# A higher rank for mLSTM work in the emission order of a hybrid decoder step

## The chip, the cores and the metric

The kernel runs on one core of a Trainium2 chip. The metric is the device time of one execution in microseconds, from the program's first to its last instruction with what the launch adds around it. "Before" was run three times; one more execution was recorded by the profiler.

## The reference

One layer of an autoregressive decoder is computed for a prompt of 512 positions and for 8 samples of one position each, 520 rows in all, with shared weights:

```
z = rmsnorm(h) @ w_in                      # 1024 -> 8456 columns
o_a = dilated sliding-window attention(z)  # 12 heads; samples read cached keys and values
o_b = mlstm(conv(z)) * sigmoid(z_o)        # 4 heads of 256; samples carry a state C of 256 x 256
h += (sig(g_a) * (o_a @ w_proj_a) + sig(g_b) * (o_b @ w_proj_b)) @ w_out
h += (silu(x @ w_gate) * (x @ w_up)) @ w_down        # x = rmsnorm(h)
h += sigmoid(rmsnorm(h) @ w_ple_gate) * (p @ w_ple_proj)
y = rmsnorm(h)
```

Outputs are y, the new key and value caches, the convolution rows, and the mLSTM state (C, n, m) of prompt and samples. For one sample and head the new state is C' = x·C + k (w v)ᵀ, and the numerator of its output is C'ᵀ q. The output o_b of a head needs the prompt half (512 columns) and the sample half (8 columns).

## The kernel before, in words

All 520 rows stand on the free axis, split in two halves of 260 columns, and features stand on the partitions. Each weight tile of 128 x 128 is split into a rounded part and a remainder (`whi` by ACT or DVE, `wlo` by DVE), and each activation likewise, so that one product is three matmuls. The weights of the projections stream through in a fixed order of chunks (`order`): the columns of `w_in` (attention of the first head pair, mLSTM head 0, attention of the second pair, heads 1 to 3, output gates, then the gate columns g), then `w_proj_a` and `w_proj_b`, `w_out`, and the feed-forward part. `w_proj_b` and most of the feed-forward part use a seven-product block scheme (`wino`), whose right sides are sums of halves of two activation tiles. The tiles that hold them are called `piece`; for `w_proj_b` the four mLSTM heads give them, one after the other (`mk_ob`), and the first block product walks through all four heads.

Everything beside the dense products is written as Python generators. Each yields a condition (`on(engine, tiles, rooms)`: the engine's queue reaches not more than LIM past TensorE's, the tiles are ready, buffers of the named tags are free), by a clock that the kernel keeps while it emits instructions. This clock has costs of its own: a transfer, for one, is taken to land 2.0 us after its turn on the queue. `Procs.run()` is called several times in each chunk of the dense work. In such a turn it goes through the list of evacuations (`evs`) and then through the list `live`, each from its front, and lets each generator go on as long as its condition holds. Weight splits (`feed`) come before it in the turn. So the place in the list decides who takes a free place on an engine; the engines' own queues then run in the order of emission.

The list `live` in the kernel before, from the front: first norm, attention chain of the prompt (`attn_prompt(0)`, then `(1)`; its eight units each are spawned while it runs and go to the end of the list), the mLSTM prompt chain (`mlstm_prompt(0)` to `(3)`), the sample attention (`samples`), the samples' loads (`loads`, head by head; head 0 first, heads 1 to 3 after the sample attention has issued its last value loads, flag `vs`), `sample_rows`, `mlstm_sample`, then `mk_oa` and `mk_ob` (spawned before the dense work starts), and behind them whatever is spawned later: attention units, the two step generators of each head (`steps(0)` for even samples, `steps(1)` for odd ones), `sample_sums`, and the stores of results.

For one mLSTM head the sample half goes so: `sample_rows` writes q and k of the 8 samples to DRAM (`mdr`). `sample_loads` loads q and k of a pair of samples back, spread over the partitions, into one buffer of P1 and one of P2 (`qb`, `kb`; each tag has 2 buffers), and for each sample the state `ct` into one of the 5 buffers of S. A step scales `ct` (ACT or DVE), adds k·v (`ct<-kb,vw,ct`, DVE, twice), multiplies by q and sums (`junk<-ct,qb` into `numv`, DVE, twice), and stores `ct`. When both samples of a pair are done their P1 and P2 buffers come free for the next pair but one. After 8 samples `sample_sums` and `sample_out` multiply the head's tanh gates `th` by `numv`. The prompt half ends with the product `th<-th,hm`. With both, `mk_ob` scales `th` and makes the head's pieces; for head 3 it needs all 5 buffers of S.

P1 and P2 serve attention too: each unit keeps its scores `P` there. Later the gate columns g of two of every four rounds go to P1 and P2, and their evacuation waits until the loads of head 3 have all been issued:

```
if tag in ("P1", "P2"):
    yield lambda: ("loads", 3) in flag
```

All operations are recorded by one helper, so every row of the profile has line 225; rows are told apart by tiles.

Of the kernel before, what the change touches and what calls it, by code (L numbers as in the profile page):

```python
# [229 lines left out]
def _body(nc, a, const, sb, psp, drp):  # L230
# [10 lines left out]
    def tl(tag, name, shape=None, dt=F32):  # L241
        w = WIDTH.get(tag, 520)
        if tag in used:
            used[tag] += 1
        return ck.new(sb.tile(list(shape or (128, w)), dt, name=name, tag=tag, bufs=NB[tag]), tag, NB[tag])
# [8 lines left out]
    def bank(shape=(128, 512)):  # L254
        used["b1"] += 1
        return ck.new(psp.tile(list(shape), F32, name="b1", tag="b1", bufs=4), "b1", 4)
# [7 lines left out]
    def free(n, tag):  # L264
        used[tag] -= n
# [5 lines left out]
    def on(engs, *tiles, lim=None, **rooms):  # L271

        engs = engs.split()

        def ok():
            for tag, n in rooms.items():
                if tag in used and used[tag] + n > NB[tag]:
                    return False
            now = ck.t["pe"]
            for tag, n in rooms.items():  # L280
                i = ck.count.get(tag, 0)
                if any(ck.idle(tag, i + j, NB[tag]) > now + P["SLACK"] for j in range(n)):
                    return False
            if engs[0] == "pe":
                t = now
            else:
                t = min(ck.t[e] for e in engs)
                if t > now + (P["LIM"] if lim is None else lim):
                    return False
                t = max(t, now) + 0.1  # L290
            return all(ck.ready(x) <= t for x in tiles)
        return ok

    class Cycle:
        def __init__(self, tags):
            self.tags, self.i = tags, 0

        def next(self, n):
            return [self.tags[(self.i + k) % len(self.tags)] for k in range(n)]
# [4 lines left out]

    class Procs:
        def __init__(self):
            self.evs, self.live = [], []

        def spawn(self, gen, first=False):
            (self.evs if first else self.live).append([None, gen])  # L310

        def run(self):
            for q in (self.evs, self.live):
                for p in list(q):
                    while p[0] is None or p[0]():
                        try:
                            p[0] = next(p[1])
                        except StopIteration:
                            q.remove(p)
                            break  # L320

    pr = Procs()
# [24 lines left out]
    def pick(names, op, out, ins):  # L347
        def end(n):
            aps = [out] + ins
            s, cost = ck.start(n, [out], ins), ck.cost(n, op, out, aps, ())  # L350
            if ck.shares(n, op, aps):
                s, _ = ck.port(s, cost)
            return s + cost + (P["BIAS"] if n == "dve" else 0.0)
        return min(names, key=end)
# [3 lines left out]
    def copy(dst, src, names=("act", "dve")):  # L358
        n = pick(names, "tensor_copy", dst, [src])
        if n == "act":  # L360
            S_.copy(dst, src)
        else:
            ENG[n].tensor_copy(dst, src)
# [5 lines left out]
    def stt(dst, x, sc, y, op0, op1):  # L369
        V.scalar_tensor_tensor(dst, x, sc, y, op0=op0, op1=op1)  # L370
# [956 lines left out]
    def sample_rows(h):  # L1327

        yield lambda: all(("k", h, dt) in ml for dt in range(2)) and "rows" in flag
        yield on("pe", qkm, b1=1, S=1)  # L1330
        bk = bank((8, 2, 2, 128))
        rows = tl("S", "mrows", (8, 2, 256))
        for w in range(2):
            for dt in range(2):
                PE.transpose(bk[:, w, dt], qkm[:, h, w, dt], ident)
        yield on("act dve", bk)
        copy(rows.rearrange("b w d -> b (w d)"), bk.rearrange("b w t d -> b (w t d)"))
        free(1, "b1")
        yield on("sp", rows)
        dr = drp.tile([8, 2, 256], F32, name="mdr", tag="mdr", bufs=2)  # L1340
        SP.dma_start(dr.rearrange("b w d -> b (w d)"), rows.rearrange("b w d -> b (w d)"))
        free(1, "S")
        mdr[h] = dr
# [18 lines left out]
    def mlstm_sample(h):  # L1362
        yield lambda: (h, 0) in cts and all(("v", h, vt) in ml for vt in range(2))
        yield on("dve", vm, s24b)
        vw = sb.tile([128, 2, 8], F32, name="vw", tag="vw", bufs=2)
        V.tensor_tensor(vw, vm[:, h], s24b[:, h, 8:16].unsqueeze(1).to_broadcast([128, 2, 8]), op=ALU.mult)
        numv = sb.tile([128, 2, 8], F32, name="numv", tag="numv", bufs=2)
        left = [8]

        def steps(b0):  # L1370
            for b in range(b0, 8, 2):
                yield lambda: (h, b) in cts
                cur = cts.pop((h, b))
                qb, kb = qks[h, b - b % 2]
                yield on("act dve", cur, s24b)
                if pick(("act", "dve"), "tensor_scalar", cur, [cur]) == "act":
                    S_.activation(cur, cur, AF.Copy, scale=s24b[:, h, b:b + 1])
                else:
                    V.tensor_scalar(cur, cur, s24b[:, h, b:b + 1], None, op0=ALU.mult)
                for vt in range(2):  # L1380
                    yield on("dve", cur, kb, vw)
                    stt(cur[:, vt], kb[:, b % 2], vw[:, vt, b:b + 1], cur[:, vt], ALU.mult, ALU.add)
                for vt in range(2):
                    yield on("dve", cur, qb)
                    V.tensor_tensor_reduce(junk, cur[:, vt], qb[:, b % 2], 1.0, 0.0, ALU.mult, ALU.add,
                                           numv[:, vt, b:b + 1])
                left[0] -= 1
                done[b] = True
                if b ^ 1 in done:
                    free(1, "P1")  # L1390
                    free(1, "P2")
                store(a["C_s"][h, b], cur, lambda: free(1, "S"))

        done = {}
        for b0 in range(2):
            pr.spawn(steps(b0))
        yield lambda: left[0] == 0
        pr.spawn(sample_sums(h, numv))

    def sample_sums(h, numv):  # L1400

        nn = nout[:, h, :, 1:9]
        w_i = s24b[:, h, 8:16].unsqueeze(1).to_broadcast([128, 2, 8])
        w_x = s24b[:, h, 0:8].unsqueeze(1).to_broadcast([128, 2, 8])
        nt = small(32, "nt").rearrange("p (t c) -> p t c", t=2)
        tv = nt[:, :, 0:8]
        V.tensor_tensor(tv, qkm[:, h, 1], w_i, op=ALU.mult)
        V.tensor_tensor(nn, nst[:, h], w_x, op=ALU.mult)
        V.tensor_tensor(nn, nn, tv, op=ALU.add)
        V.tensor_tensor(tv, nn, qkm[:, h, 0], op=ALU.mult)  # L1410
        V.tensor_tensor(nt[:, :, 8:16], numv, numv, op=ALU.mult)
        yield on("pe", nt, b1=1)
        bk = bank((128, 16))
        for t in range(2):
            PE.matmul(bk, ones, nt[:, t], start=t == 0, stop=t == 1)

        dn = sb.tile([128, 16], F32, name="dns", tag="dns", bufs=2)
        yield on("act", bk)
        S_.activation(dn[:, 0:8], bk[:, 0:8], AF.Abs)
        V.tensor_copy(dn[:, 8:16], bk[:, 8:16])  # L1420
        free(1, "b1")
        yield on("dve", dn)
        V.tensor_tensor(dn[:, 0:8], dn[:, 0:8], s24b[:, h, 16:24], op=ALU.max)
        ml["ns", h] = True
        yield lambda: ("og", h, 0) in ml and ("og", h, 1) in ml
        yield from sample_out(h, numv, dn)
# [163 lines left out]
    def chain(*gens):  # L1590
        for g in gens:
            yield from g
# [113 lines left out]
    def loads():  # L1706
        for c in "0a123":
            if c == "a":
                yield lambda: "vs" in flag
            else:  # L1710
                yield from sample_loads(int(c))
# [4 lines left out]
    for c in "apm":  # L1716
        if c == "a":
            pr.spawn(chain(attn_prompt(0), attn_prompt(1)))
        elif c == "p":
            pr.spawn(chain(*[mlstm_prompt(h) for h in range(4)]))  # L1720
        else:
            pr.spawn(samples())
            pr.spawn(loads())
            pr.spawn(chain(*[sample_rows(h) for h in range(4)]))
            pr.spawn(chain(*[mlstm_sample(h) for h in range(4)]))

    oa = []

# [393 lines left out]
    for h in range(2):  # L2122
        pr.spawn(last_norm(h))
    dense_to(len(order))
    while pr.evs or pr.live:
        stall()
    while copies:
        cache_copy()
# [141 lines left out]
```

## Time and profile before

| | |
|---|---|
| three runs | 1102.45, 1105.98, 1107.39 us; median 1105.98 |
| the profiled execution | 1104.25 us, span 1102.5 us from first to last instruction |
| TensorE busy | 1050.2 us |
| DVE busy | 859.1 us |
| ACT busy | 522.8 us |
| mean granted clock of TensorE | 0.979 of full speed |

Times in the rows are microseconds from the span's start. PE is TensorE's matmul, PEld its weight load, DVE VectorE, ACT ScalarE, SPq the queue on which SyncE issues transfers. A row of a timeline has start, length, engine, line, operation, out<-in with shapes, and the count of merged instructions; in brackets stands the engine's idle time just before and what ended it. The granted clock is 1.00 at 2.4 GHz and 0.50 at 1.2 GHz.

### The profile page before, as it was taken

To read this page: it belongs to the slowest core of one execution; us is meant where nothing else is said; L and a number is where in the kernel's file an instruction comes from. 1 tells how busy PE (TensorE), PEld (TensorE's weight loads), DVE (VectorE), ACT (ScalarE), POOL (GpSimd) and SP (SyncE) were. 2 spreads that over 40 slices of the span, in tenths; PEclk is the share of its full clock that TensorE was granted. 3 is DMA by queue.
4 is the path that set the end of the run, shared out by engine and by line. 5 is a ranking of instruction groups with operands and counts; after the bars stand their busy time and mean duration, and the time that the engine had idled before them with its cause. 6 is when DMAs were issued, how large, how long until landed. Compare 5 with 4: busy or idle time off the path is not lost.

```text
span 1102.5 us, 21771 instructions
## 1 busy us (share of the span) xinstructions
PE 1050.2 (95%) x8404; PEld 1026.4 (93%) x8404; DVE 859.1 (78%) x1768; ACT 522.8 (47%) x968; POOL 35.8 (3%) x126
## 2 busy tenths in 40 slices
PE   7999999999998999997999999989999999999995
PEld 6999899999998989996999999989999999999995
DVE  7994559877778599876466868999888888866775
ACT  6445444664454487754343335435344434433553
POOL 0010010001001011000000000000000000000000
PEclk9999999999997999998999999999999999999998
DMA  6365157747846986876566833322323332333321
GB/s 229 118 201 174 58 193 244 269 150 227 269 138 218 309 268 197 268 213 227 197 210 233 283 103 96 121 84 92 103 83 108 111 101 83 110 94 97 120 83 59
DMA packets 90904, 180.21 MB, mean 163 GB/s; under 512 B 11604, under 2 KB 37252, under 8 KB 89392
## 3 DMA queue, kind: packets, MB, share of 16 engines
q1 hardware_dynamic: 90800, 178.82, 50.5%
q8 instruction: 66, 1.08, 0.4%
q14 instruction: 38, 0.31, 0.1%
HBM read 163.65 MB, written 59.13 MB: 202 GB/s over the span
## 4 chain that ended last, share of the span: by engine, by line
PE 67%; DVE 15%; DMA 8%; ACT 5%; issue 3%; SPq 1%; POOL 0%; DVEq 0%; ACTq 0%
PE pp L225 42%; PE b L225 25%; DVE wlo L225 3%; DMA raw<-in_w_in 3%; DVE yc L225 2%; ACT whi L225 2%; DMA out_C_s<-ct 1%; DMA ct<-in_sC 1%; DMA qb<-mdr 1%; DVE ct L225 1%; SPq L225 1%; DVE junk L225 1%; DVE piece L225 1%; DVE sw L225 1%; DVE h L225 1%
## 5 line engine op out<-in xcount | busy, mean ns | idle before, releaser
L225 DVE TENSOR_TENSOR wlo<-raw,whi 128x512 fp32r<-128x512 f32 (+3 forms) x358 | 236.6, 664 | 148.1 <-ACT whi L225 134.5
L225 ACT CAST whi<-raw 128x512 fp32r<-128x512 f32 (+3 forms) x340 | 203.1, 601 | 290.8 <-PE pp L225 155.3
L225 PE MATMUL b<-piece,whi 128*128 128x260 f32 x1232 | 229.3, 287 | 10.0 <-ACT piece L225 6.0
L225 PE MATMUL pp<-xnh,whi 128*128 128x260 f32 x1008 | 209.4, 289 | 0.8 <-ACT th L225 0.8
L225 PE MATMUL pp<-xnh,wlo 128*128 128x260 f32 x1008 | 208.4, 288 | 0.0
L225 PEld LDWEIGHTS b<-piece,whi 128*128 128x128 f32 x1232 | 194.5, 193 | 12.1 <-ACT piece L225 6.7
L225 PE MATMUL pp<-xnl,whi 128*128 128x260 f32 x1008 | 204.8, 285 | 0.8 <-DVE xnl L225 0.7
L225 PE MATMUL b<-piece,wlo 128*128 128x260 f32 x616 | 176.7, 287 | 0.1
L225 PEld LDWEIGHTS pp<-xnh,whi 128*128 128x128 f32 x1008 | 157.4, 191 | 2.2 <-ACT th L225 1.0
L225 PEld LDWEIGHTS pp<-xnl,whi 128*128 128x128 f32 x1008 | 157.9, 191 | 1.2 <-DVE xnl L225 1.2
L225 PEld LDWEIGHTS pp<-xnh,wlo 128*128 128x128 f32 x1008 | 157.4, 191 | 1.1
L225 PEld LDWEIGHTS b<-piece,wlo 128*128 128x128 f32 x616 | 118.6, 193 | 0.6 <-DVE wlo L225 0.6
L225 PE MATMUL pp<-hpl,whi 128*128 128x260 f32 x352 | 70.8, 282 | 0.0
L225 PE MATMUL pp<-hph,whi 128*128 128x260 f32 x352 | 70.8, 282 | 0.0
L225 PE MATMUL pp<-hph,wlo 128*128 128x260 f32 x352 | 70.7, 282 | 0.0
L225 PEld LDWEIGHTS pp<-hpl,whi 128*128 128x128 f32 x352 | 54.2, 188 | 0.0
L225 PEld LDWEIGHTS pp<-hph,wlo 128*128 128x128 f32 x352 | 54.2, 188 | 0.0
L225 PEld LDWEIGHTS pp<-hph,whi 128*128 128x128 f32 x352 | 54.2, 188 | 0.0
L225 ACT CAST whi<-ws 128x512 fp32r<-128x512 f32 x29 | 17.9, 621 | 57.1 <-PE b L225 48.5
L225 DVE TENSOR_TENSOR uv<-uv,b 128x260 f32<-128x260 f32 (+1 forms) x88 | 42.7, 485 | 0.0
L225 DVE SCALAR_TENSOR_TENSOR yc<-zc,par,yc 128x552 f32<-128x552 f32 x48 | 37.8, 788 | 5.0 <-ACT yc L225 4.5
L225 PE MATMUL pp<-mix,whi 128*128 128x260 f32 x256 | 41.1, 282 | 0.0
(383 smaller groups left out, 1875.3 us busy)
## 6 DMA issues: line engine op xcount, KB each, us to landing
raw<-in_w_in SPq DMA_DIRECT2D x132, 256.0 KB, 3.5
out_kvout<-in_cache SPq DMA_DIRECT2D x64, 512.0 KB, 4.6
raw<-in_w_gate SPq DMA_DIRECT2D x44, 256.0 KB, 3.6
raw<-in_w_up SPq DMA_DIRECT2D x44, 256.0 KB, 4.4
ct<-in_sC SPq DMA_DIRECT2D x32, 256.0 KB, 6.6
out_C_s<-ct SPq DMA_DIRECT2D x32, 256.0 KB, 4.4
raw<-in_w_down SPq DMA_DIRECT2D x32, 256.0 KB, 2.6
out_kvout<-in_cache SPq DMA_DIRECT2D x16, 510.0 KB, 4.9
```

The source lines that it names most:

```text
L225: fn(*args, **kw)
```

## The change

The scheduler gets a third list, `urgent`, between the evacuations and `live`. The prompt chain, the samples' loads, rows and per-head chain, the step generators and the samples' sums are spawned into it. The sample attention, the attention chain and its units, `mk_oa`, `mk_ob` and the stores stay in `live`. Within `urgent` the order is: prompt chain, loads, rows, per-head chain, then steps and sums as they are spawned.

```diff
     class Procs:
         def __init__(self):
-            self.evs, self.live = [], []
-
-        def spawn(self, gen, first=False):
-            (self.evs if first else self.live).append([None, gen])
+            self.evs, self.urgent, self.live = [], [], []
+
+        def spawn(self, gen, first=False, urgent=False):
+            (self.evs if first else self.urgent if urgent else self.live).append([None, gen])
 
         def run(self):
-            for q in (self.evs, self.live):
+            for q in (self.evs, self.urgent, self.live):
...
         for b0 in range(2):
-            pr.spawn(steps(b0))
+            pr.spawn(steps(b0), urgent=True)
         yield lambda: left[0] == 0
-        pr.spawn(sample_sums(h, numv))
+        pr.spawn(sample_sums(h, numv), urgent=True)
...
         elif c == "p":
-            pr.spawn(chain(*[mlstm_prompt(h) for h in range(4)]))
+            pr.spawn(chain(*[mlstm_prompt(h) for h in range(4)]), urgent=True)
         else:
             pr.spawn(samples())
-            pr.spawn(loads())
-            pr.spawn(chain(*[sample_rows(h) for h in range(4)]))
-            pr.spawn(chain(*[mlstm_sample(h) for h in range(4)]))
+            pr.spawn(loads(), urgent=True)
+            pr.spawn(chain(*[sample_rows(h) for h in range(4)]), urgent=True)
+            pr.spawn(chain(*[mlstm_sample(h) for h in range(4)]), urgent=True)
...
-    while pr.evs or pr.live:
+    while pr.evs or pr.urgent or pr.live:
         stall()
```

## Rows read from the trace of the kernel before

**Rows 1.** The page, part 1: busy time, share of the span, instructions.

```profile
PE 1050.2 (95%) x8404; PEld 1026.4 (93%) x8404; DVE 859.1 (78%) x1768; ACT 522.8 (47%) x968; POOL 35.8 (3%) x126
```

**Rows 2.** Busy time by stretch: length, engines (instructions), granted clock, DMA share, GB/s.

```profile
440.00:450.00 10.00, 10.00 (x78) 9.74 (x77) 7.15 (x18) 6.11 (x12) 0.00 (x0) 1.00 1.00 346
...
490.00:497.50 7.50, 7.50 (x65) 7.50 (x64) 1.85 (x3) 1.49 (x3) 0.00 (x0) 1.00 0.77 210
...
514.00:526.10 12.10, 9.18 (x39) 7.86 (x40) 9.13 (x17) 4.69 (x9) 0.00 (x0) 0.58 0.26 87
...
497.50:530.50 33.00, 24.94 (x164) 22.79 (x163) 20.86 (x55) 14.24 (x26) 0.00 (x0) 0.84 0.54 185
530.50:556.50 26.00, 26.00 (x219) 26.00 (x218) 12.62 (x21) 10.32 (x18) 0.00 (x0) 1.00 0.77 272
```

**Rows 3.** Waits from 497 to 531 us: total, times, longest.

```profile
PE b L225 <- ACT piece L225: 4.7, 2, 2.8
...
PE pp L225 <- ACT th L225: 2.6, 3, 1.0
```

**Rows 4.** Timeline of PE: first product on pieces, and the last that waited.

```profile
510.28 0.40 PE L225 MATMUL b<-piece,whi 128*128 128x260 f32 x2
...
522.90 0.59 PE L225 MATMUL b<-piece,whi 128*128 128x260 f32 x1 [0.15 <-DVE piece L225]
```

**Rows 5.** Timeline of SP's queue: second and last pair of head 3.

```profile
451.62 0.38 SPq L225 DMA_DIRECT2D qb<-mdr  x1
...
491.45 1.45 SPq L225 DMA_DIRECT2D qb<-mdr  x1
```

**Rows 6.** Timeline of DVE: steps of heads 2 and 3, and their gate products.

```profile
415.86 0.36 DVE L225 CUSTOM_DVE_ANT_0 junk<-ct,qb 128x256 bf16<-128x256 f32 x1
...
432.57 0.42 DVE L225 CUSTOM_DVE_ANT_0 junk<-ct,qb 128x256 bf16<-128x256 f32 x1
...
465.37 1.67 DVE L225 SCALAR_TENSOR_TENSOR ct<-kb,vw,ct 128x256 f32<-128x256 f32 x4
...
483.79 0.42 DVE L225 CUSTOM_DVE_ANT_0 junk<-ct,qb 128x256 bf16<-128x256 f32 x1
...
484.13 0.68 DVE L225 SCALAR_TENSOR_TENSOR th<-th,hm 128x512 f32<-128x512 f32 x1
...
507.18 0.42 DVE L225 CUSTOM_DVE_ANT_0 junk<-ct,qb 128x256 bf16<-128x256 f32 x1
...
512.41 0.24 DVE L225 SCALAR_TENSOR_TENSOR th<-th,numv 128x8 f32<-128x8 f32 x2
```

**Rows 7.** Tile ct: duration ns min/median/max, first and last start.

```profile
L225 DVE SCALAR_TENSOR_TENSOR ct<-kb,vw,ct x64: 384/479/491, 167.7 to 504.4; 128x256 f32<-128x256 f32 x64
L225 DVE CUSTOM_DVE_ANT_0 junk<-ct,qb x64: 360/422/428, 169.7 to 507.2; 128x256 bf16<-128x256 f32 x64
...
L225 ACT ACTIVATE ct<-ct,s24b x31: 705/722/730, 163.9 to 501.4; 128x512 f32<-128x512 f32 x31
...
DMA to landing us min/median/max: 2.1/6.0/7.2
```

**Rows 8.** Tile piece alone, by stretch: length, PE, PEld, DVE, ACT.

```profile
460.00:470.00 10.00, 0.00 (x0) 0.00 (x0) 3.57 (x7) 0.93 (x2) 1.00 0.56 183
470.00:480.00 10.00, 0.00 (x0) 0.00 (x0) 2.56 (x5) 0.62 (x1) 1.00 0.73 220
```

**Rows 9.** Tiles P and qb: attention's scores, the sample attention's key products.

```profile
L225 DVE CUSTOM_DVE_ANT_0 P<-b,cstA x32: 284/418/425, 92.5 to 244.0; 128x256 f32<-128x256 f32 x28, 128x128 f32<-128x128 f32 x4
...
L225 DVE TENSOR_TENSOR kvb<-kvb,qb x12: 679/684/693, 244.5 to 301.1; 128x512 f32<-128x512 f32 x12
```

**Rows 10.** Timeline of ACT: waits for transfers at the head of its queue.

```profile
364.10 1.40 ACT L225 ACTIVATE ct<-ct,s24b 128x512 f32<-128x512 f32 x2 [2.85 <-DMA out_C_s<-ct]
...
448.42 0.62 ACT L225 CAST whi<-raw 128x512 fp32r<-128x512 f32 x1 [3.21 <-DMA raw<-in_w_in]
```

**Rows 11.** Busy time by stretch, as rows 2: the costliest stall before 400 us.

```profile
345.00:355.00 10.00, 6.87 (x37) 6.35 (x37) 9.37 (x23) 4.77 (x9) 0.41 (x1) 0.67 0.30 108
```

## The prediction

> **What bounds the kernel now.** I read the page's busy times first: TensorE (PE) is recorded busy for 95% of the span [rows 1], so a gain can come only from the few stretches in which it stands or runs slowly. The busy times by stretch find the one that this change can reach. Between 497.5 and 530.5 us TensorE gets through 164 matmuls in 33.0 us; in the 26.0 us behind it, with the same kind of work (gate columns, two short products, seven block products), 219 [rows 2]. That is 26.0 / 219 = 0.1187 us each, and 164 × 0.1187 = 19.5 us: the stretch loses 33.0 − 19.5 = **13.5 us**. Part of it is standing still: three waits of 2.6 us together for ACT's `th` and two of 4.7 us for ACT's `piece` [rows 3]. The rest is mainly clock: behind the long wait, from 514 to 526.1 us, the granted clock is 0.58 on average, mostly its lower level of 1.2 GHz, and 39 matmuls take 12.1 us [rows 2].
>
> The timelines then tell who is late. TensorE reaches the first product on `piece` at 510.28 us and gets the last piece that it lacks at 522.90 [rows 4]. The pieces are those of the fourth mLSTM head, and they wait for its sample half: the last sample's `junk` (the numerator) is made at 507.18, the tanh gates are multiplied by it at 512.41 [rows 6], then scaling and splitting take to 522.90. Before it stands a load: the last pair of samples is issued on the SP queue at 491.45, where the second pair went at 451.62 [rows 5]. That issue needs a buffer of P1 and one of P2, which come free when both samples of an earlier pair are done. The second pair's update (`ct<-kb,vw,ct` x4) ran at 465.37, but its last `junk`, a 0.42 us instruction that needs nothing more, ran at 483.79 [rows 6]: 17 us in which the step was passed over. The three `th` waits are of the same origin: tanh gates that go to P1 and P2 may not be evacuated before the loads of head 3 are all issued.
>
> **The change part by part.** No instruction is added or removed; only the order of emission can differ.
>
> *Prompt chain, sample rows, loads.* In the list of before they stand behind the first norm, the attention chain and (all but the prompt chain) the sample attention, but ahead of the attention units, which are spawned later and go to the list's end. What they are lifted over is seldom alive beside them: attention's `P` is written from 92.5 to 244.0 and the sample attention's key products run from 244.5 to 301.1 [rows 9], while the chain of waits of interest begins after 430. Cost taken: 0 us, with a reason for no large sign: where nobody else has a condition that holds, rank decides nothing. The SP issues of the loads pass only the sample attention's, which end before head 1's loads start by the code's own condition (`vs`).
>
> *Steps.* They stood at the list's end, behind `mk_oa` and `mk_ob`, which are spawned at the start and come alive when the last head's projections are done. Now they go ahead of both. A step is one scaling (0.72 us on ACT), two updates (0.48 us) and two `junk` (0.42 us) with two 0.08 us read-outs: 2 × 0.48 + 2 × 0.42 + 0.16 = 2.0 us of DVE [rows 7]. What they pass between 460 and 480 us is pieces of heads 1 and 2, 3.57 + 2.56 = 6.1 us of DVE [rows 8], besides their sums `ta` and `tb`. These pieces are not wanted before 507; moved back, they are hidden by DVE's idle time from 490 to 497.5, where it is busy 1.85 of 7.5 us [rows 2]. Without that cover they would stall TensorE by up to their 6.1 us, which I keep as a bound.
>
> *What the last pair gains.* From its issue to TensorE's release it is 522.90 − 491.45 = 31.4 us. TensorE without the three `th` waits would want the pieces at 510.28 − 2.6 = 507.7, so the issue must come by 476.3 for the whole stall to go. If the steps win only the time of the pieces that they pass, the issue moves to 491.45 − 6.1 = 485.4, and the release to 516.8: the low bound. If the second pair's `junk` follow its updates as soon as DVE has a place, they end near 469 instead of 484.2, the issue comes near 470, and the release near 501.4: the stall is gone. I take the second, since at 465 to 484 the steps' only rivals above them besides the pieces are the prompt chain's own end and the weight splits, and both go on anyway.
>
> *What is late next.* The prompt half of head 3: its last gate product stands at 484.13 (0.68 us long) [rows 6]. From there scaling and pieces, which took 522.90 − 512.41 = 10.5 us in the sample's case, end at 495.3, still 12 us ahead of 507.7. So TensorE itself is next.
>
> *Loads that come earlier.* A pair is four transfers of 256 KB, pulled forward into a stretch where the DMA engines are already full: share 1.00 from 440 to 450 [rows 2]. There ACT waited 3.21 us for a weight tile at 448.42 [rows 10], and TensorE was busy 10.00 of 10 us all the same [rows 2]. Cost taken 0; upper bound one stall as from 345 to 355 us, where 37 matmuls were done in 10 us instead of 10 / 0.1187 = 84: 47 × 0.1187 = 5.6 us, lower clock included [rows 11].
>
> Sum: −13.5 us, plus 1.5 us that I leave for the new hand-overs (half of the 3 us by which the waits for ACT there could come back), = **−12 us**.
>
> **A rule weighed.** Rows 1 name TensorE as the busiest engine by far. The Trainium skill, Perfetto Trace Analysis, section Identifying the Most-Contended Engine, says to improve the engine of highest occupancy first; by it a new order of DVE and ACT work would leave 1104 us. The same page's section Optimization Strategy asks for the gaps of the regime in question and for what blocks there, and by it the stall is fair game; the rows of the stretch agree with the second.
>
> **The rivals.**
> *Half of it: the top ranks hold the steps.* Evacuations, weight splits and the prompt chain stay ahead. For it: between 415.86 and 432.57 two neighbouring `junk` lie 16.7 us apart [rows 6], before any piece is written. Against it: that was the convolutions' time, and their evacuations end around 430. Then only the 6.1 us of the low bound are won: 1104.25 − 6.1, about 1098 us.
>
> *Nothing.* The last pair stays behind the same weight loads on the SP queue, or another late thing (the pieces of heads 0 to 2, now behind the steps) takes the stall's place in full. Against it, the 12 us of room above. Time 1104 to 1106 us.
>
> *Slower: waits at the head of the queues.* The emission's clock reckons that a transfer lands 2.0 us after its time on the queue; `ct` landed after 6.0 us (median) and up to 7.2 [rows 7]. A step of the last rank was put in its queue late, when the data was there; one of a higher rank is put in at once and stands there, with weight splits behind it. At 364.10 such a scaling held ACT for 2.85 us, put down to the store that its buffer waited for [rows 10]. The place is 440 to 480 us, four pairs, and a stall of TensorE costs 5.6 us [rows 11]. From 12 / 5.6 = 2.1 stalls on the gain is eaten; with all four, 22.4 − 12 = +10, 1115 us. Against it: steps of heads 1 and 2 ran without a competitor from the list and so were put in at once too, and ACT's waits there delayed TensorE little. The Trainium skill (Perfetto Trace Analysis, Tensor Engine Instruction) calls ACT and DVE strict FIFOs, which this mechanism needs; ACT's wait at 448.42 agrees.
>
> **How the numbers follow.** The profiled execution took 1104.25 us (span 1102.5); 1104.25 − 12 = 1092.3. The median of the three runs is 1.7 us higher, which gives 1094.0; I say 1093. Chances: whole stall gone 0.60 (1088 to 1097), half 0.16 (about 1098), nothing 0.13 (1104 to 1106), slower 0.11 (1107 to 1115). The range 1087 to 1107 leaves out only most of the last case and the best ends of the first. About 0.5%, 5.5 us, is what a measurement can tell. Below 1100.5 lie the first case and most of the second: faster 0.70; what is left of the second and the third: same 0.19; slower 0.11.
>
> **What would show it.** Right: stretches up to 430 us nearly as before; the last `qb<-mdr` issued before 476 instead of 491; the last gate product with `numv` before 495; the first product on pieces near 508 with no wait over 1 us behind it and no lower clock up to 530; everything later shifted by some 12 us. Half: that issue near 485, and a wait for `piece` of 5 to 9 us. Slower: waits of ACT or DVE for `ct` of 2 us and more between 440 and 480, with a lower clock there. I should be wrong if the order changes before 300 us, where I found nobody to be passed, or if a weight tile comes too late for TensorE in the fuller DMA stretch.

## The result, and the profile after

| | before | after |
|---|---|---|
| median of 4 runs | 1105.58 us (1102.45 to 1107.39) | 1088.82 us (1087.17 to 1090.90) |
| profiled execution | 1104.25 us, span 1102.5 | 1088.87 us, span 1087.1 |
| mean granted clock | 0.979 | 0.991 |

The ratio is 0.9855, 95% interval 0.9834 to 0.9877: faster by 1.45%, 16 us of 1105.58. The same changed kernel in a second job gave 1094.12 us against 1107.55, ratio 0.9882 (0.984 to 0.9925), and three parts measured beside it are read against that.

First the page of after, busy time by engine, to be held against [rows 1].

```profile
PE 1039.2 (96%) x8404; PEld 1016.2 (93%) x8404; DVE 859.3 (79%) x1772; ACT 520.2 (48%) x964; POOL 37.0 (3%) x126
```

The 8404 matmuls are the same, and their recorded busy time has fallen by 1050.2 − 1039.2 = 11.0 us. So most of the 15.4 us by which the span is shorter had been counted as work of TensorE. That fits the lower clock, of which there is less: a mean of 0.979 over 1102.5 us stands for 46 us at 1.2 GHz, 0.991 over 1087.1 us for 20.

The same stretches as [rows 2, 11] show where.

```profile
345.00:355.00 10.00, 4.59 (x21) 4.32 (x22) 9.77 (x29) 4.10 (x7) 0.41 (x1) 0.56 0.28 93
...
440.00:450.00 10.00, 10.00 (x79) 9.74 (x80) 8.33 (x30) 7.06 (x12) 0.00 (x0) 1.00 1.02 331
...
490.00:497.50 7.50, 7.50 (x65) 7.50 (x64) 6.33 (x14) 6.47 (x12) 0.00 (x0) 1.00 0.66 198
...
497.50:530.50 33.00, 33.00 (x277) 33.00 (x277) 20.75 (x36) 12.29 (x22) 0.00 (x0) 1.00 0.62 214
...
530.50:556.50 26.00, 26.00 (x220) 26.00 (x218) 17.65 (x31) 9.61 (x19) 0.00 (x0) 1.00 0.69 233
...
514.00:526.10 12.10, 12.10 (x103) 12.10 (x103) 9.22 (x16) 4.14 (x7) 0.00 (x0) 1.00 0.71 240
```

The stretch from 497.5 to 530.5 holds 277 matmuls where it held 164, at a clock of 1.00, as dense as the one behind it (33.0 / 277 = 0.119 us each; 26.0 / 220 = 0.118). From 514 to 526.1 it is 103 in place of 39. DVE's idle time from 490 to 497.5 is mostly used up: it is busy 6.33 us of 7.5 where it was 1.85. The stretch from 345 to 355 is still bad, with 21 matmuls at a clock of 0.56 where there were 37 at 0.67.

Then the sample half of head 3: the timeline of SP's queue, second and last pair [rows 5], and of DVE [rows 6].

```profile
441.35 0.57 SPq L225 DMA_DIRECT2D qb<-mdr  x1
...
461.43 0.58 SPq L225 DMA_DIRECT2D qb<-mdr  x1
```

```profile
454.96 1.66 DVE L225 SCALAR_TENSOR_TENSOR ct<-kb,vw,ct 128x256 f32<-128x256 f32 x4
...
457.62 0.41 DVE L225 CUSTOM_DVE_ANT_0 junk<-ct,qb 128x256 bf16<-128x256 f32 x1
...
459.42 0.43 DVE L225 CUSTOM_DVE_ANT_0 junk<-ct,qb 128x256 bf16<-128x256 f32 x1
...
473.74 1.66 DVE L225 SCALAR_TENSOR_TENSOR ct<-kb,vw,ct 128x256 f32<-128x256 f32 x4
...
478.07 0.36 DVE L225 CUSTOM_DVE_ANT_0 junk<-ct,qb 128x256 bf16<-128x256 f32 x1
...
487.89 0.68 DVE L225 SCALAR_TENSOR_TENSOR th<-th,hm 128x512 f32<-128x512 f32 x1
...
488.93 0.24 DVE L225 SCALAR_TENSOR_TENSOR th<-th,numv 128x8 f32<-128x8 f32 x2
```

The second pair's `junk` now stand right behind their updates (454.96, then 457.62 to 459.42), and the last pair is issued 2 us later, at 461.43 instead of 491.45. Its updates run at 473.74, its last `junk` at 478.07, and the gates of head 3 are multiplied by `numv` at 488.93 instead of 512.41, 1 us behind the last product of the prompt half (487.89). TensorE's timeline, first product with `oah` and first with `piece`:

```profile
502.84 0.40 PE L225 MATMUL pp<-oah,whi 128*128 128x260 f32 x2
...
505.71 0.40 PE L225 MATMUL b<-piece,whi 128*128 128x260 f32 x2
```

TensorE waits for nothing at all from 497 to 531 us, where [rows 3, 4] had waits for `th` and `piece`. The chain of work that ended last (start, length, link) agrees. Its longest link outside TensorE behind 460 us is a state on its way in; short links on ACT and DVE follow, the last of them at 479.55, and from there to the block products TensorE stands in the chain alone.

```profile
462.57 7.37 DMA ct<-in_sC
...
479.55 0.18 DVE nt L225
...
480.39 25.48 PE pp L225 x212
505.88 10.05 PE b L225 x84
```

Three milestones divide the difference of the spans. Up to the first product with `oah` it is 502.8 − 505.7 = −2.9 us; from there to the first product with `mix`, behind all block products of `w_proj_b`, 603.4 − 502.8 = 100.6 against 618.9 − 505.7 = 113.2, that is −12.6; from there to the end 483.7 against 483.6.

### The profile page after: what moved, and what is told of

Its sections match the earlier page's. It is cut to its first block, busy times and chain, and to the rows that moved or that the text cites. A ratio compares the mean times of both kernels' runs of the same rounds, so it can differ in the third digit from the quotient of the medians.

```text
span 1087.1 us, 21770 instructions
## 1 busy us (share of the span) xinstructions
PE 1039.2 (96%) x8404; PEld 1016.2 (93%) x8404; DVE 859.3 (79%) x1772; ACT 520.2 (48%) x964; POOL 37.0 (3%) x126
## 4 chain that ended last, share of the span: by engine, by line
PE 69%; DVE 16%; DMA 7%; ACT 4%; issue 3%; SPq 1%; POOL 0%; DVEq 0%; ACTq 0%
PE pp L225 45%; PE b L225 24%; DVE wlo L225 3%; DMA ct<-in_sC 2%; DVE yc L225 2%; DVE ct L225 1%; ACT whi L225 1%; DMA raw<-in_w_in 1%; DMA out_C_s<-ct 1%; SPq L225 1%; DVE junk L225 1%; DMA kvb<-in_cache 1%; DMA out_kvout<-in_cache 1%; DVE sw L225 1%; DVE Wf L225 1%
## 5 line engine op out<-in xcount | busy, mean ns | idle before, releaser
L225 PE MATMUL b<-piece,whi 128*128 128x260 f32 x1232 | 224.5, 284 | 4.6 <-DVE piece L225 1.5
L225 PEld LDWEIGHTS b<-piece,whi 128*128 128x128 f32 x1232 | 190.9, 189 | 5.4 <-issue 2.0
## 6 DMA issues: line engine op xcount, KB each, us to landing
out_kvout<-in_cache SPq DMA_DIRECT2D x64, 512.0 KB, 5.1
```

The lines of the kernel that those rows point to most:

```text
L225: fn(*args, **kw)
```

## The experiments

Each run also shows one profiled execution. For all of them the same two numbers are taken from its timelines: the *lead*, from the issue of the last `qb<-mdr` to the first product with `piece`, and the *stretch*, from that product to the first with `mix`.

| kernel | ratio to before, 95% interval | issue | first `piece` product | lead | stretch |
|---|---|---|---|---|---|
| before | 1 | 491.45 | 510.3 | 18.8 | 108.6 |
| hold_late | 0.9978 [0.9949, 1.0007] | 492.85 | 513.5 | 20.7 | 103.8 |
| ob_urgent | 0.9920 [0.9902, 0.9938] | 484.98 | 506.4 | 21.4 | 105.1 |
| no_steps | 0.9978 [0.9948, 1.0008] | 484.74 | 506.3 | 21.6 | 105.8 |
| hold_3 | 0.9867 [0.9823, 0.9910] | 479.95 | 506.4 | 26.4 | 98.5 |
| hold_mid | 0.9873 [0.9834, 0.9911] | 484.40 | 514.4 | 30.0 | 99.4 |
| chain_first | 0.9909 [0.9884, 0.9934] | 469.11 | 505.8 | 36.7 | 100.1 |
| ob_last | 0.9912 [0.9880, 0.9943] | 478.04 | 519.7 | 41.7 | 99.0 |
| rows_live | 0.9865 [0.9831, 0.9899] | 465.52 | 508.9 | 43.4 | 97.5 |
| after_again | 0.9882 [0.9840, 0.9925] | 465.16 | 509.2 | 44.0 | 98.5 |
| after | 0.9855 [0.9834, 0.9877] | 461.43 | 505.7 | 44.3 | 97.7 |
| prompt_steps | 0.9898 [0.9856, 0.9941] | 462.01 | 509.8 | 47.8 | 97.6 |
| steps_first | 0.9927 [0.9899, 0.9955] | 468.69 | 516.7 | 48.0 | 98.6 |
| prompt_live | 1.0017 [0.9998, 1.0036] | 462.94 | 516.1 | 53.2 | 106.2 |

**Are the steps the cause?** In no_steps they stay in `live`, and all else is promoted.

```diff
-            pr.spawn(steps(b0), urgent=True)
+            pr.spawn(steps(b0))
```

> Changed kernel, but the two step generators of each head stay at the end of the live list (behind mk_oa and mk_ob); prompt chain, loads, rows, per-head chain and sums stay promoted. Theory (the gain is the steps' place ahead of the pieces of heads 0 to 2): the stall before the first block products returns, the last qb<-mdr is issued near 490 us again, waits for ACT piece of 4 us and more with a lower clock behind them, total 1100 to 1105 us. Rival A (the gain comes from the other promotions, or from stores being seen in the same turn): the stall stays away, 1087 to 1091 us. Rival B (any reshuffle of the order moves the stall by chance): anywhere between, with the last issue at a place that has nothing to do with the pieces.

Measured: 1104.22 us (1097.14 to 1109.06), nearly all of the gain gone. The profiled execution is the fastest of the ten; in it the last pair goes out at 484.74 and not near 490 as expected, and the waits for pieces sum to 3.4 us and not to 4 and more. SP's and TensorE's timelines show the last pair and two of these waits.

```profile
484.74 0.42 SPq L225 DMA_DIRECT2D qb<-mdr  x1
...
509.05 0.39 PE L225 MATMUL b<-piece,whi 128*128 128x260 f32 x1 [1.42 <-DVE piece L225]
...
512.40 0.59 PE L225 MATMUL b<-piece,whi 128*128 128x260 f32 x1 [0.87 <-DVE piece L225]
```

**Is it the place relative to the pieces?** In ob_last nothing is promoted, but `mk_oa` and `mk_ob` go to a list of their own behind `live`; in ob_urgent all is promoted as in the change, and these two also, ahead of the steps.

```diff
# ob_last, against before
-            for q in (self.evs, self.live):
+            for q in (self.evs, self.live, self.late):
...
-    pr.spawn(mk_oa())
-    pr.spawn(mk_ob())
+    pr.spawn(mk_oa(), late=True)
+    pr.spawn(mk_ob(), late=True)
# ob_urgent, against after
-    pr.spawn(mk_oa())
-    pr.spawn(mk_ob())
+    pr.spawn(mk_oa(), urgent=True)
+    pr.spawn(mk_ob(), urgent=True)
```

> Kernel before with one thing else: mk_oa and mk_ob go to a third list behind live, so that the steps pass them although nothing is promoted. Theory: this alone gives the gain, 1088 to 1093 us, last qb<-mdr near 462 to 470 us, no wait for piece over 1 us before 570 us; the order up to 430 us is that of before. Rival A (other promotions): 1102 to 1106 us. Rival B (chance): between.

> Changed kernel with mk_oa and mk_ob promoted too; being spawned before the steps they stand ahead of them again, while everything else is as in the changed kernel. Theory: the steps are passed over between 460 and 484 us as before, the last qb<-mdr comes after 480 us, total 1098 to 1104 us. Rival A: 1087 to 1091 us.

Measured: 1096.89 us (1094.14 to 1107.77) and 1098.07 us (1096.38 to 1099.07), against 1106.25. To move two generators back wins 9 us without any promotion, of the 16 and 13 that the changed kernel won in its two jobs, and its stretch is as short as that of after. It was expected at 1088 to 1093 us with the issue at 462 to 470. Its profiled execution is the slowest of the ten and has head 3's write of q and k (`mdr<-mrows`) at 442.65 instead of 427.04; counted from that write the issue comes after 35.4 us, as in after (34.4) and not as in before (58.8). Where the rest of the gain stays is open. To move the two up in the changed kernel brings the issue back to 484.98 and the stretch to 105.1.

**Is it the date of the last pair?** hold_late, hold_3 and hold_mid keep the order of the changed kernel and hold only the last pair's loads until the loads of weights have come to a given chunk.

```diff
                 yield on("sp", dr, P1=1, P2=1)   # before this line:
+                if h == 3 and b == 6:
+                    yield lambda: dma_at[0] > n_win        # hold_late
+                    yield lambda: dma_at[0] > n_win - 3    # hold_3 instead
+                    yield lambda: dma_at[0] > n_win - 5    # hold_mid instead
```

> Changed kernel in which the last pair of head 3 may be loaded only after the first weight chunk of w_proj_a has been requested, which is where the kernel before had it (near 491 us); the order of everything else is left to the lists. Theory (the issue of this pair sets TensorE's release some 28 to 31 us later): the stall returns with release near 520 us, that is 520 - 506 = 14 us of wait and lower clock at most, total 1098 to 1103 us, although the pieces of heads 0 to 2 are no different. Rival C (the gain is relief of DVE and ACT in general, not this chain): below 1093 us.

> The changed kernel with the last pair of head 3 held back until a chunk of the dense work five before the end of the gate columns, so that its issue should come between 475 and 481 us instead of at 461. Theory: the release of the last piece follows 31.4 us behind the issue, and TensorE wants the pieces at about 505, so an issue before 474 costs nothing and each microsecond behind it about one, plus the lower clock once the wait is long enough: with an issue at 478 the time is 1089 to 1094 us, against 1103.7 with the issue at 492.9. Rival (what helps is the early issue as such, or the emptier queues behind it, not the date at which the pieces are wanted): half or more of the gain is lost, 1096 us and above.

> The changed kernel with the last pair of head 3 held back until a chunk of the dense work three before the end of the gate columns: between the run that held it to five before the end (issue 49.3 us behind the last write of q and k, no loss) and the one that held it to the end (62 us, 15 us lost). Theory (release 31.4 us behind the issue, TensorE wants the pieces 78.5 us behind that write, so each microsecond behind 47 to 50 is lost, with the lower clock on top once the wait is some microseconds long): with the issue at 53 to 58 us behind the write, TensorE waits 3 to 8 us altogether, 1096 to 1102 us. Rival (nothing is lost until a threshold near the end): 1092 to 1095 us.

Measured: 1103.74 us, 1093.70 us and 1092.36 us. One date, put back, takes nearly the whole gain with it. hold_late's timelines (SP, then TensorE) show the waits of before again, and the 33.0 us from 497.5 hold only 184 matmuls.

```profile
492.85 0.43 SPq L225 DMA_DIRECT2D qb<-mdr  x1
...
517.00 1.05 PE L225 MATMUL b<-piece,whi 128*128 128x260 f32 x2 [2.25 <-ACT piece L225]
...
523.38 0.39 PE L225 MATMUL b<-piece,whi 128*128 128x260 f32 x1 [1.70 <-ACT piece L225]
```

```profile
497.50:530.50 33.00, 26.07 (x184) 24.87 (x183) 21.35 (x55) 14.61 (x28) 0.00 (x0) 0.90 0.54 190
```

Against after, hold_late's span is 15.2 us longer. 3.7 us of that lie ahead of head 3's write of q and k, before the hold acts (430.76 against 427.04). From there to the first product with `oah` it is 4.0 us more, 2.6 of them waits for `th`, from that product to the first with `mix` 6.2 (106.8 against 100.6), and behind it 1.4. So this run tests the date of the pair's loads with all that hangs on it: the evacuation of the gate columns that go to P1 and P2 is held with them.

hold_mid came out as expected in its time, but its issue is later than the 475 to 481 us that were meant, its execution was late throughout (head 3's write of q and k at 435.06), and its lead is 30.0 us. hold_3 missed its expectation of 3 to 8 us lost: nothing measurable is lost with the issue at 479.95, and of the pieces none was waited for. Its timelines (SP, TensorE, DVE):

```profile
479.95 0.43 SPq L225 DMA_DIRECT2D qb<-mdr  x1
...
504.87 0.51 PE L225 MATMUL pp<-oah,whi 128*128 128x260 f32 x2 [1.64 <-ACT th L225]
...
506.39 0.40 PE L225 MATMUL b<-piece,whi 128*128 128x260 f32 x2
...
500.00 0.24 DVE L225 SCALAR_TENSOR_TENSOR th<-th,numv 128x8 f32<-128x8 f32 x2
...
508.81 0.69 DVE L225 TENSOR_TENSOR piece<-tb,piece 128x520 fp32r<-128x520 f32 x1
```

The last piece, that of the sum `tb`, begins only at 508.81, 2.4 us behind the first product with `piece`, and nobody waits for it. So between a lead of 26.4 and one of 21.6 us the stretch goes from 98.5 to 105.8: 5 us less lead cost 7. Each of these figures is from one execution.

The lead is not the whole of it, for chain_first, below, has 36.7 us and still waits for a piece. Counted from the last sample's `junk` to the first product with `piece` the runs fall in line. Before has 3.1 us, no_steps and ob_urgent have 7.5 and hold_late 8.8, with waits for pieces of 3.4 to 4.8 us in sum; chain_first has 12.5 and waits 2.4 us; hold_3 has 13.1 and waits for none, like all those with 14 us and more. The exception is prompt_live, where the other half is late. In chain_first this `junk` comes 24 us behind the issue, at 493.32, and in after 17; why is open.

**Which promotions are needed?** prompt_steps promotes only the prompt chain and the steps. prompt_live promotes all but the prompt chain, rows_live all but the rows.

```diff
# prompt_steps: loads, sample_rows, mlstm_sample, sample_sums back to live
-            pr.spawn(loads(), urgent=True)
+            pr.spawn(loads())
...
# prompt_live
-            pr.spawn(chain(*[mlstm_prompt(h) for h in range(4)]), urgent=True)
+            pr.spawn(chain(*[mlstm_prompt(h) for h in range(4)]))
# rows_live
-            pr.spawn(chain(*[sample_rows(h) for h in range(4)]), urgent=True)
+            pr.spawn(chain(*[sample_rows(h) for h in range(4)]))
# after_again: no edit
```

> The changed kernel once more, unchanged, so that the parts beside it have it on their own chip. Theory (the whole stall before the block products of w_proj_b is gone, worth some 11 to 13 us from the first product with oah to the first with mix, and 3 to 5 us come from stretches before 430 us): 1087 to 1091 us. Rival (the 3 us before 430 us are chance of the execution, since the stretch around 350 us varies by 3 us at the same order): 1089 to 1094 us, with milestones before 430 us as late as the kernel before has them.

> The changed kernel with the sample rows (the transposes and the writes of q and k) left in the last list; all else urgent. It asks what the 6.00 us wait of TensorE for qkm of GpSimd at 349.56 us in the changed kernel is worth. Theory (the rows' transposes are put into TensorE's queue earlier by their rank and wait there for the slow GpSimd product, but the stall only replaces another one of the same stretch): the wait is 2 us or shorter, the stretch from 330 to 385 us has within 4 of its 354 matmuls, time 1087 to 1091 us. Rival (the rank of the rows costs the whole wait): 1083 to 1086 us, the best version so far. Second rival (the rows' rank brings the gain before 430 us): 1091 to 1094 us, first pair of head 3 issued at 436 to 439 us instead of 431.

> Only the prompt chain and, behind it, the steps are urgent; the loads, the rows, the per-head chain and the sums stay in the last list as in the kernel before. Theory (the pair prompt chain, then steps is what the change lives on; the rest only shifts some transfers by a few microseconds): last pair issued at 460 to 470 us, no wait for a piece over 1 us, 1088 to 1095 us, from the first product with oah to the first with mix 100 to 102 us. Rival (the loads' rank is needed too: in the last list they come behind the pieces and the attention units, so that the last pair's issue waits for its turn although its buffers are free): issue after 476 us, waits for th or piece again, 1096 to 1103 us.

> The changed kernel with the prompt chain of the mLSTM left in the last list; loads, rows, per-head chain, steps and sums stay urgent. Theory (the steps' place ahead of the pieces does the work; the prompt chain has little to pass): last pair issued at 455 to 466 us, no wait for pieces over 1 us, 1088 to 1092 us. Rival 1 (the prompt chain's rank brings the 3 to 5 us before 430 us): 1092 to 1095 us, with the last write of q and k of head 3 again near 432.7 us instead of 427.0. Rival 2 (with steps ahead of it the prompt half becomes the late one): the last product of th and hm comes after 495 us and TensorE waits for pieces, 1093 us and above.

Measured: after_again 1094.12 us, rows_live 1092.74, prompt_steps 1096.38, prompt_live 1109.28. The rows' rank does nothing to the time that can be told from no change. Without it head 3's first pair goes out at 439.37 (434.82 in after_again), as the second rival of that run had it, but TensorE reaches the first product with `oah` no later, at 506.1 against 506.3. The pair of prompt chain and steps is not told from the whole change either (intervals 0.9856 to 0.9941 and 0.9840 to 0.9925). Its 1096.38 us lie at the lower edge of the rival's range, but its issue, at 462.01, and its 100.4 us from `oah` to `mix` are those of the theory. But prompt_live is no faster than before, although its last pair goes out at 462.94. DVE's and TensorE's timelines show the other half of head 3's output as the late one:

```profile
522.19 0.69 DVE L225 SCALAR_TENSOR_TENSOR th<-th,hm 128x512 f32<-128x512 f32 x1
...
523.48 1.05 PE L225 MATMUL b<-piece,whi 128*128 128x260 f32 x2 [6.16 <-DVE piece L225]
```

The prompt half ends at 522.19 instead of 487.89, and TensorE waits 6.16 us for a piece: rival 2 of that run. That is not the whole loss. Against after_again, the same job's, its span is 14.8 us longer. Of these 8.9 lie between `oah` and `mix` (110.3 against 101.4), and 5.7 ahead of the first product with `oah` (512.0 against 506.3).

**Why does the prompt chain have to stay in front?** Both runs keep all members of the changed kernel's urgent list and alter its order: steps_first puts the steps to the front, chain_first the loads, rows and per-head chain.

```diff
# steps_first
-            pr.spawn(steps(b0), urgent=True)
+            pr.urgent.insert(b0, [None, steps(b0)])
# chain_first (the rows at 1 and the per-head chain at 2 likewise)
-            pr.spawn(loads(), urgent=True)
+            pr.urgent.insert(0, [None, loads()])
```

> The changed kernel with the same members in the urgent list, but the step generators put at its front, ahead of the prompt chain, as they stand relative to it in the run that left the prompt chain in the last list. Theory (it was the steps ahead of the prompt chain that made the prompt half of head 3 late there, its last product of th and hm at 522 us): the last product of th and hm comes at 515 to 525 us, TensorE waits 4 us and more for a piece, 1102 to 1110 us. Rival (it was the attention chain ahead of the prompt chain): that product stays near 488 to 495 us, no wait over 1 us, 1088 to 1096 us.

> The changed kernel with the same members in the urgent list, but the loads, the rows and the per-head chain of the samples put ahead of the prompt chain; steps and sums stay behind it. With the prompt chain in the last list two things went wrong: some 9 us were lost before 375 us, which the steps ahead of the prompt chain alone also did, and the prompt half of head 3 came 35 us late, which the steps alone did not do. Theory (rows and per-head chain ahead of the prompt chain make its last head late): the last product of th and hm comes at 505 to 522 us, TensorE waits 3 us and more for a piece, nothing is lost before 375 us, 1096 to 1104 us. Rival (it takes the prompt chain behind all of them, or behind attention in the last list): that product stays at 486 to 495 us, no such wait, 1088 to 1095 us.

Measured: 1100.48 us and 1094.64 us. In neither does the prompt half of head 3 come as late as 522 (500.26 and 488.88), so both theories fell, though chain_first did not keep its rival's "no such wait" either. steps_first has its short stretch, 98.6 us, and loses ahead of it: its last product with attention's `P` stands at 257.7 us (248.4 before, 247.1 after) and its first product with `oah` at 513.8. prompt_live has that product with `P` at 257.1 too, so the steps ahead of the prompt chain are common to the two early losses. chain_first loses little, with a wait of 2.08 us for a piece. What makes the prompt half 34 us late in prompt_live takes more than either of these orders by itself. It was not settled.

## Why the prediction was right

The predicted 1093 us stand against 1088.8 in the first job and 1094.1 in the second; both lie in the range.

*The stall and its chain.* Right in its links: the passed-over step of the second pair, the buffers of P1 and P2, the last pair's issue, the gates, the pieces. no_steps and hold_late each cut one link of it and lose nearly all of the gain; ob_last makes the link by another edit and gets more than half of it. Two readings in it were off. The `junk` at 483.79 is not the second pair's last. The program emits, after the four updates at 465.37, both `junk` of sample 2, the updates of sample 4, the first `junk` of sample 3, both of sample 4, and only then the second of sample 3. In DVE's timeline of before that is the one at 485.80, so it was passed over for 19 us and not 17, at the end also by sample 4 of the third pair: the generator of the even samples stands in front of that of the odd ones. From its end the issue took 5.2 us more, behind loads of weights on SP's queue; in after it took 1.6.

```profile
485.80 0.43 DVE L225 CUSTOM_DVE_ANT_0 junk<-ct,qb 128x256 bf16<-128x256 f32 x1
```

```profile
490.50 0.34 SPq L225 DMA_DIRECT2D raw<-in_w_pa  x1
...
491.45 1.45 SPq L225 DMA_DIRECT2D qb<-mdr  x1
```

The other is the `th` waits. They were put down to the flag that the loads of head 3 are issued. But a gate column for P1 or P2 also needs a free buffer there, and the last pair holds its own until its last `junk`. ACT's timelines show it waiting for that, in before and in chain_first, whose loads had all been issued by 471.2:

```profile
507.65 0.60 ACT L225 ACTIVATE th<-pp 128x520 f32<-128x520 f32 x1 [2.00 <-DVE numv L225]
```

```profile
493.79 0.60 ACT L225 ACTIVATE th<-pp 128x520 f32<-128x520 f32 x1 [0.62 <-DVE numv L225]
```

*The size.* 13.5 us less 1.5 for hand-overs was predicted. The waits for ACT did not come back at all, so the allowance was not needed; −12.6 us were measured from `oah` to `mix`, besides the waits of 0.76 and 0.97 us for `th` that end ahead of it and went too.

*The date of the issue.* "Near 470" became 461.43, with head 3's write of q and k already 5.7 us early in this execution (427.04 against 432.70). The deadline of 476.3 was too strict. It came from comparing the release of the last piece (522.90) with the first product that reads any piece; the pieces of the sums are read by later block products, and hold_3 shows an issue at 479.95 in time. The error made no difference, because the real issue was far ahead of both.

*The half case* was priced at about 1098 with the issue at 485.4. ob_urgent has its issue at 484.98 and takes 1098.07. no_steps has it at 484.74 and takes 1104.22 in the median, though 1097.14 in its profiled execution, its fastest; why these two differ is not settled.

*The pieces moved back.* Hidden, as argued from DVE's idle time. From 460 to 480 us fewer of them run than in [rows 8], and some of heads 0 to 2 now run from 480 to 490, where the kernel before had none. The tile `piece` alone, by stretch:

```profile
460.00:470.00 10.00, 0.00 (x0) 0.00 (x0) 1.68 (x3) 1.57 (x3) 1.00 0.79 266
470.00:480.00 10.00, 0.00 (x0) 0.00 (x0) 1.25 (x3) 0.41 (x1) 1.00 0.56 182
480.00:490.00 10.00, 0.00 (x0) 0.00 (x0) 1.68 (x3) 1.69 (x3) 1.00 0.67 223
```

*The prompt half is next.* It was put at 484.13, pieces ready at 495.3; it came at 487.89, 4 us later through the steps now in the way, and the last piece, from 497.11, ends at 497.8. The room held. prompt_live shows what it is worth: with the prompt half at 522.19 most of the gain between `oah` and `mix` is gone (110.3 us, where after_again has 101.4 and before 113.2).

*Waits at the head of the queues*, the slower rival. The steps are indeed put into their queues early, and from 430 to 490 ACT and DVE each wait for a `ct` (total, times, longest), but by about 1 us, where 2 us and more each would have been needed.

```profile
ACT ct L225 <- DMA ct<-in_sC: 0.9, 2, 0.7
...
DVE ct L225 <- DMA ct<-in_sC: 1.2, 1, 1.2
```

Over the whole program the waits for a state's load do grow, from 14.7 us in 6 waits to 23.9 us in 12, and four of the 32 scalings go from ACT to DVE; no loss from it shows in the whole time. The landing time that this rival was reckoned with is also a mixture: of the transfers in [rows 7] only nine have a known landing, five of them stores; the four loads landed after 5.9 to 7.2 us.

The rival showed itself at another place: the transposes of `qkm`, promoted with the rows, stand at the head of TensorE's queue for 6.00 us in the profiled execution of after and for 3.51 in after_again (1.59 before).

```profile
349.56 0.38 PE L225 MATMUL b<-cstA,qkm 128*8 128x128 f32 x1 [6.00 <-POOL qkm L225]
...
352.09 1.08 PE L225 MATMUL b<-cstA,yc 128*128 128x128 f32 x4 [0.86 <-DVE nout L225]
```

```profile
352.48 0.27 PE L225 MATMUL b<-cstA,qkm 128*8 128x128 f32 x1 [3.51 <-POOL qkm L225]
...
355.01 1.09 PE L225 MATMUL b<-cstA,yc 128*128 128x128 f32 x4 [1.55 <-DVE nout L225]
```

rows_live has 1.83 us there and is not measurably faster, 0.9865 against 0.9882. From 330 to 385 us it has 341 matmuls, against 354 in after, 358 in after_again and 356 in before; within 4 of 354 had been expected. So without that wait the 55 us come out no fuller, and the wait costs nothing that shows.

*"Up to 430 us nearly as before".* The order does change a little before 300 us, which the prediction named as a ground for being wrong, for example in stores that go out a turn earlier; the write of head 1's q and k moves only from 286.38 to 285.89 us. The 2.9 us won up to `oah` were not predicted. after_again, the same program, has its first product with `oah` at 506.3 us, 0.6 later than before, and everything behind it as in after: its `oah` to `mix` takes 607.7 − 506.3 = 101.4 us. So these 2.9 us are within what one execution differs from the next, and the 12 to 13 us from `oah` to `mix` are what both executions of the changed kernel share.

*The rule weighed.* The rows of the stretch decided rightly against the busy shares. By the Trainium skill (Perfetto Trace Analysis, Identifying the Most-Contended Engine) the busy share of matmuls is not a good measure of how close TensorE is to its roofline. The trace agrees as far as it goes, since TensorE was 95% busy before and is 96% busy after, with 11.0 us less in it.

## What to carry to other kernels

Where a program is emitted by generators that poll in a fixed order, look for a short instruction that had its data long before it ran, and follow what its buffer holds back: here 0.42 us of DVE work, 19 us late, decided when a load was issued whose result was wanted 20 to 30 us later. A product that needs two halves is won only if the rank of both is kept; promoting the later half past the earlier one left the time where it was (prompt_live). And before promoting a whole list of things, try to move back the one or two that are in the way: that alone brought 9 us, where the whole change brought 13 to 16.

## What the runs showed of the hardware

The granted clock differs between executions of the same instructions. hold_mid is the changed kernel in all that is issued ahead of its held loads, and at 304 us the same matmul starts 0.14 us apart in the two executions (304.42 and 304.28). From 304 to 311 us TensorE does nearly the same in both, first after and then hold_mid:

```profile
304.00:311.00 7.00, 6.01 (x46) 5.51 (x44) 6.83 (x19) 3.13 (x9) 0.13 (x1) 1.00 0.12 39
```

```profile
304.00:311.00 7.00, 5.96 (x45) 5.47 (x44) 6.83 (x20) 3.12 (x9) 0.27 (x3) 1.00 0.16 46
```

From 311 to 328 us hold_mid then has the lower clock, 1.2 GHz, and after has not. From 305 to 335 us after has:

```profile
305.00:335.00 30.00, 28.97 (x233) 28.16 (x233) 22.87 (x47) 16.14 (x27) 1.79 (x12) 1.00 0.49 151
```

and hold_mid:

```profile
305.00:335.00 30.00, 28.96 (x166) 27.79 (x165) 15.46 (x35) 12.90 (x22) 0.89 (x6) 0.72 0.35 104
```

That is a mean of 0.72 and 67 matmuls fewer in 30 us. The write of head 3's q and k, still ahead of any difference, stands at 427.04 in after and at 435.06 in hold_mid. Single executions of one order can so be 8 us apart ahead of the place under study, which is why stretches between milestones were compared here and not only whole times.

DMA engines that were already full took the earlier loads without holding TensorE: share 1.02 from 440 to 450 us, TensorE busy 10.00 of 10 us.

And lateness is not paid one for one. Below a lead of some 26 us, 5 us less cost 5 to 7 in the stretch (no_steps, ob_urgent, hold_late), of which only part is waiting: in before the waits for pieces sum to 4.9 us, the stretch is 10 to 11 us longer than in after, and the granted clock behind the first wait is 0.58 [rows 2].
